# Attention of 48 steps in one sequence, both heads' scores side by side, and input weights split by an accumulating DMA

## The chip, the cores and the metric

The kernel runs on one core of a Trainium2 chip. The metric is the device time of one execution in microseconds (us), the median of several runs. The engines are TensorE (PE; its weight loads are listed apart as PEld), VectorE (DVE), ScalarE (ACT), GpSimd (POOL) and SyncE (SP). SP and POOL issue the DMAs, each in the order in which they stand in its own instruction stream.

## The reference, cut to what matters

One layer of a decoder trunk is computed for a prompt of 1024 tokens and 8 single-token samples, 1032 columns in all, with 1024 channels. One combined projection of the normalised input feeds a convolution branch, an attention branch and two gates:

```python
h = rms_norm(x, g_mix)
z = h @ w_in                                    # w_in: 1024 x 6400
a_lin, a_gate, q, k, v, g_a, g_b = jnp.split(z, SPLITS, axis=-1)
u = a_lin * jax.nn.sigmoid(a_gate)
c, new_conv = causal_dwconv(hist_conv, u, w_dw, b_dw)           # width 31
out_a = jax.nn.silu(layer_norm(c, ln_g, ln_b)) @ w_conv_out
q = rope(q.reshape(n_seq, t_len, N_HEADS, HEAD_DIM), pos) * (HEAD_DIM ** -0.5)
k = rope(k.reshape(n_seq, t_len, N_HEADS, HEAD_DIM), pos)
# three groups of four heads, window 128/512/2048, dilation 1/4/16:
s = jnp.einsum('brnqhd,brnkhd->brnhqk', qb, kb)                 # masked to the band
mx = jnp.max(s, axis=-1, keepdims=True)
p = jnp.exp(s - mx)
den = jnp.sum(p, axis=-1, keepdims=True)
o = jnp.einsum('brnhqk,brnkhd->brnqhd', p, vb) / den
# groups are weighted by their softmax sums, then out_b = o @ w_attn_out
x = x + (sigmoid(g_a) * out_a + sigmoid(g_b) * out_b) @ w_out
# then RMSNorm, the gated ConvFFN (up, conv of width 3, SiLU, down), residual, final RMSNorm
```

Each head has 64 channels, so two heads fill the 128 partitions of one block of q, k or v.

## The kernel before, in words

**Products.** Every large product is made of three passes in fp32r. A weight block of 128x1024 (`raw`) is split into a rounded high part `hi` and a rest `lo`; the activations are split likewise (`hh`, `hl`). `product` (L203) then adds `hi`·`hh`, `hi`·`hl` and `lo`·`hh` for eight channel blocks, 24 matmuls of 344 columns into one PSUM bank. `mm_blocks` (L219) makes three such banks, 3 x 344 columns, for one block of output channels; "job" below means one such weight block with its 72 matmuls. The pools hold `raw` twice and `hi` and `lo` three times (`WB` = 3), so a weight block can be split when the job three before it has ended.

**Loading weights.** `load_w` (L190) fetches `raw` from SP's queue; `split_w` (L180) makes `hi` by a copy on ACT and `lo = raw - hi` by a subtraction on DVE, with a raised priority.

**The stages.** After the first products come the input projections of the convolution, `ag` and `al` in turn (8 blocks each). A convolution of 31 taps for each of 8 channel blocks runs on DVE (`conv_wide`, L494: `ca<-cu,c_w_dw,ca`) from then until the gates. Then six attention units follow, numbered b = 0 to 5 (head group g = b // 2, pair of heads p = b % 2), each with a job of `q`, `k` and `v`; then the gates `ga` and `gb` (8 jobs each), the attention's output product `ob`, and the rest of the layer.

**Order.** `mm_blocks` calls `pump` (L125) after each bank: it takes steps from the queues `later` (attention), `second` and `third` (combining the groups, layer norm, the samples' output) and `taps` (convolution). So the source interleaves small work with the large products; from there a scheduler places each engine's instructions. `anchor` (L155) ties taps on DVE behind the last step of the work that PE needs.

**One attention unit.** `attention_unit` (L570) evacuates q, k and v on ACT, turns q and k by `rope` (L538: a STREAM_SHUFFLE and three or four operations of 1032 columns on DVE), and splits the 1024 tokens into eight blocks i = 0 to 7. `s20` is the score tile of unit 2, block 0. For each block there are three PE parts. `scores` (L603): for each of the two heads one score product in a bank of its own (tag `s`, two banks), each followed on DVE by a reduction that adds the mask and finds the maximum (`sm<-s`), and then one `nm` (minus the maximum) and two exponentials on ACT (`pr`). `turn` (L623): two or four transposes of the probabilities (`pt`), copied by ACT to `pk`. `weigh` (L633): two or four products with the values (`o`), copied by ACT to `ot`. `step(t)` of a unit (L644) runs `weigh(t-2)`, `turn(t-1)` and `scores(t)`, ten steps for a unit. These parts are in plain f32 and stand between the fp32r matmuls of the projections. `values` transposes v in two banks of tag `t`; the samples' scores (`products`, L676) use the bank of tag `o`.

## Time and profile before

| | us |
|---|---|
| time before, median of 3 runs (1661.45 to 1664.89) | 1663.66 |
| the profiled execution's own time | 1660.85 |
| its span in the trace | 1659.1 |
| PE busy in the span | 1616.9 |
| DVE busy | 1148.3 |
| ACT busy | 611.2 |
| POOL busy | 149.0 |

The span runs from the first to the last instruction of the profiled execution. A busy share is a mean over stages with different limits; a stretch of the trace says which engine was full there. A matmul's row gives its start and a modelled duration; since matmuls overlap, the cost of one is read from start to start.

### The profile page before, as it was taken

The page shows a single profiled execution, that of the slowest core. Times are in us where ns is not written, and L with a number is a line of the kernel's source. Part 1 is how long each engine was busy: PE and PEld are TensorE (multiplying, and loading weights), DVE is VectorE, ACT ScalarE, POOL GpSimd, SP SyncE. Part 2 cuts the span into 40 slices and gives each one's busy share as a digit, 9 for nine tenths or more (in the row PEclk, how much of TensorE's full clock was granted, in tenths as well). Part 3 has the DMA queues.
Part 4 walks back from the last instruction along what each step waited for, and adds up shares of the span by engine and source line. Part 5 has one row for each costly group of instructions (what it writes and reads, how often), then busy time and mean ns, then how long its engine had stood idle before and what let it go on. Part 6 is the DMA issues. An engine that isn't in the chain of part 4 may idle for free.

```text
span 1659.1 us, 26823 instructions
## 1 busy us (share of the span) xinstructions
PE 1616.9 (97%) x11044; PEld 1572.5 (95%) x11044; DVE 1148.3 (69%) x1778; ACT 611.2 (37%) x1080; POOL 149.0 (9%) x229
## 2 busy tenths in 40 slices
PE   8999999999999999999999989999999998999997
PEld 7999998899899999999999989999999998999997
DVE  5889998798986996774435886666666667434246
ACT  6421123444434323462223354444444444311123
POOL 0110011010102102120001000000000000000002
PEclk9999999999999999999999999999999999999999
DMA  8544332322325457894453135545545546762112
GB/s 292 182 133 125 97 116 83 84 87 87 116 90 194 130 179 229 231 349 142 174 217 107 60 94 155 166 135 146 166 134 147 140 115 249 257 218 87 57 34 102
DMA packets 84393, 244.94 MB, mean 148 GB/s; under 512 B 9840, under 2 KB 31376, under 8 KB 84272
## 3 DMA queue, kind: packets, MB, share of 16 engines
q1 hardware_dynamic: 61152, 163.09, 30.1%
q0 software_dynamic: 23120, 80.15, 15.9%
q8 instruction: 86, 1.41, 0.3%
q14 instruction: 35, 0.29, 0.1%
HBM read 195.87 MB, written 92.46 MB: 174 GB/s over the span
## 4 chain that ended last, share of the span: by engine, by line
PE 77%; DMA 12%; DVE 7%; issue 2%; ACT 2%; POOL 0%; SPq 0%; DVEq 0%; POOLq 0%; ACTq 0%
PE dn L215 12%; PE qb L1086 7%; DMA sa<-w_ups 7%; PE ga L215 6%; PE oa L215 5%; PE xo L215 5%; PE v L215 4%; PE k L215 4%; PE q L215 4%; PE al L215 4%; PE ag L215 3%; PE first L215 3%; PE qc L1086 3%; PE s L612 2%; PE dl L215 2%
## 5 line engine op out<-in xcount | busy, mean ns | idle before, releaser
L502 DVE SCALAR_TENSOR_TENSOR ca<-cu,c_w_dw,ca 128x1019 f32<-128x1019 f32 (+22 forms) x240 | 300.8, 1269 | 1.7
L215 PE MATMUL dn<-gh,hi_wd 128*128 128x344 f32 x456 | 146.2, 321 | 4.8 <-DVE xs L934 4.3
L215 PE MATMUL dn<-gl,hi_wd 128*128 128x344 f32 x456 | 145.7, 320 | 0.6 <-DVE gl L68 0.6
L215 PE MATMUL dn<-gh,lo_wd 128*128 128x344 f32 x456 | 146.1, 320 | 0.0
L934 DVE TENSOR_TENSOR xs<-dn,xs 128x1032 f32<-128x1032 f32 x34 | 41.7, 1230 | 117.5 <-PE dn L215 114.7
L1068 DVE TENSOR_TENSOR sb<-sa,raw_ra 128x512 f32<-128x512 f32 x20 | 13.9, 693 | 112.8 <-DMA sa<-w_ups 111.0
L215 PEld LDWEIGHTS dn<-gh,hi_wd 128*128 128x128 f32 x456 | 85.7, 188 | 6.2 <-DVE xs L934 4.6
L215 PEld LDWEIGHTS dn<-gl,hi_wd 128*128 128x128 f32 x456 | 85.7, 188 | 1.2 <-DVE gl L68 1.2
L215 PEld LDWEIGHTS dn<-gh,lo_wd 128*128 128x128 f32 x456 | 85.7, 188 | 0.0
L68 ACT ACTIVATE hi_wd<-raw_wd 128x768 fp32r<-128x768 f32 (+1 forms) x26 | 24.2, 929 | 135.9 <-PE dn L215 130.2
L215 PE MATMUL xo<-mh,hi_wo 128*128 128x344 f32 x192 | 62.3, 325 | 3.3 <-DVE xr L962 3.3
L1086 PE MATMUL qb<-t,hi_wd 128*128 128x258 f32 x320 | 59.3, 285 | 6.3 <-DVE uv18z L1121 1.3
L1086 PE MATMUL qb<-t,hi_wc 128*128 128x258 f32 x320 | 59.8, 287 | 5.1 <-ACT s L1137 5.1
L215 PE MATMUL ga<-hh,lo_ga 128*128 128x344 f32 x192 | 62.5, 325 | 0.0
L215 PE MATMUL ga<-hh,hi_ga 128*128 128x344 f32 x192 | 62.4, 325 | 0.0
L215 PE MATMUL ga<-hl,hi_ga 128*128 128x344 f32 x192 | 62.3, 325 | 0.0
L215 PE MATMUL xo<-ml,hi_wo 128*128 128x344 f32 x192 | 62.1, 324 | 0.0
L215 PE MATMUL gb<-hl,hi_gb 128*128 128x344 f32 x192 | 62.0, 323 | 0.0
L215 PE MATMUL xo<-mh,lo_wo 128*128 128x344 f32 x192 | 61.9, 323 | 0.0
L215 PE MATMUL gb<-hh,lo_gb 128*128 128x344 f32 x192 | 61.8, 322 | 0.0
L215 PE MATMUL oa<-sl,hi_wco 128*128 128x344 f32 x192 | 61.5, 320 | 0.0
L215 PE MATMUL oa<-sh,lo_wco 128*128 128x344 f32 x192 | 61.2, 319 | 0.0
(826 smaller groups left out, 5407.9 us busy)
## 6 DMA issues: line engine op xcount, KB each, us to landing
o_k<-cache_k SPq DMA_DIRECT2D x16, 1023.5 KB, 7.4
o_v<-cache_v SPq DMA_DIRECT2D x16, 1023.5 KB, 7.4
g<-g_dram SPq DMA_DIRECT2D x22, 516.0 KB, 7.3
sa<-w_ups SPq DMA_DIRECT2D x20, 512.0 KB, 3.7
sa<-w_ups POOLq DMA_DIRECT2D x20, 512.0 KB, 6.7
raw_ra<-w_ups SPq DMA_DIRECT2D x20, 512.0 KB, 3.6
raw_wd<-w_down SPq DMA_DIRECT2D x16, 384.0 KB, 3.1
rd<-w_ups SPq DMA_DIRECT2D x20, 256.0 KB, 3.5
```

Source lines behind the costliest of these rows:

```text
L68: ins = op(*args, **kwargs)
L215: ins = nc.tensor.matmul(ps[:, :m], wk, xk, start=(k == 0 and i == 0), stop=(k == n - 1 and i == 2))
L502: after(anchor[0], nc.vector.scalar_tensor_tensor(acc[:, d:SEQ], u[:, :SEQ - d], w[:, 30 - d:31 - d], acc[:, d:SEQ], ALU.mult, ALU.add))
L612: nc.tensor.matmul(sps[:, :nk], q[hs, i * P:(i + 1) * P], k[hs, k0:k0 + nk], start=True, stop=True)
L934: nc.vector.tensor_tensor(out=v3(t), in0=ps, in1=v3(t), op=ALU.add)
L1068: nc.vector.tensor_tensor(out=s2, in0=s1, in1=ra[:, 512:], op=ALU.add)
L1086: nc.tensor.matmul(ps[:, s, :SUB], wk, xk, start=(first and k == 0 and i == 0), stop=(k == 3 and i == 2), skip_group_check=True)
```

## The change

Three things change.

**The score tiles.** The two single banks of tag `s` become one tile of two banks (`two_banks`). Both heads' score products of a block go into it, one behind the other on PE; then come the two reductions. `values` and the transposes of the attention's output (`otr`) use the same tile with eight transposes and one evacuation; the samples' scores are put right behind the next block's scores, into its first bank. The tiles of the layer norm (`lm`, `sp_lv`) take the tags `s`, `t`, `o` in turn.

**The sequence.** The ten steps of each unit become one sequence of 48 steps over all units, with three more to empty it. Step n runs `weigh(n-3)`, `turn(n-2)` and `scores(n)`, tied in this order on PE. `ready` adds waits: no `weigh` or `turn` of step n starts before the exponentials of block n-2 are done on ACT (`exps`) and `nm` of step n-1 is done on DVE (`free[0]`).

**The loads.** For the 45 weight blocks that go through `in_jobs` (`ag`, `al`, `q`, `k`, `v`, `ga`, `gb`) `load_by_dma` takes the place of `load_w`: ACT writes `hi`, and then `-raw` rounded into `lo`; a DMA of 512 KB from POOL's queue adds the weight from DRAM to it. DVE's subtraction is gone. Other weights are split as before.

```diff
-PSA = {"mm": 4, "s": 2, "t": 1, "o": 1}
+PSA = {"mm": 4, "s": 1, "t": 1, "o": 1}
...
+    def two_banks(name):
+        return psb[0].tile([P, 2, 512], F32, tag="s", name=name, bufs=1)
...
+    def ready(first, then):
+
+        tc.add_manual_dep(
+            then.ins, first.ins.name,
+            mybir.DependencyInfo(mybir.DependencyClass.Sync, mybir.DependencyReason.DATA),
+            reason="together",
+        )
...
+    def load_by_dma(src, name):
+
+        raw, d = fetch_w(src, name)
+        hi, lo = w_tiles(name)
+        with tc.high_priority(EARLY):
+            act.activation(hi, raw, AF.Copy)
+            act.activation(lo, raw, AF.Copy, scale=-1.0)
+            nc.gpsimd.dma_start(lo, src, accum_op=ALU.add)
+        paced(d)
         return hi, lo
 
...
     def in_jobs(*jobs):
-        mm_blocks([(load_w(w_in[o], name), 0, name, ev) for o, name, ev in jobs], hh, hl)
+        mm_blocks([(load_by_dma(w_in[o], name), 0, name, ev) for o, name, ev in jobs], hh, hl)
...
         def values():
-            for half in range(2):
-                ps = bank(f"vtr{b}{half}", "t")
-                for i in range(4):
-                    o = (half * 4 + i) * P
-                    nc.tensor.transpose(ps[:, i * P:(i + 1) * P], vt[:, o:o + P], ident)
-                nc.scalar.activation(v[:, half * 4:half * 4 + 4, :], ps.rearrange("p (i c) -> p i c", c=P), AF.Copy)
+            ps = two_banks(f"vtr{b}")
+            for i in range(8):
+                nc.tensor.transpose(ps[:, i // 4, i % 4 * P:(i % 4 + 1) * P], vt[:, i * P:(i + 1) * P], ident)
+            nc.scalar.activation(v, ps.rearrange("p h (i c) -> p (h i) c", c=P), AF.Copy)
...
+        def scores(i, run, extra):
             nk, k0, prev = keys(i)
             mask = mask_d if g == 2 else (mask_b if prev else mask_b[:, P:])
             sm = scratch(f"sm{b}{i}", "sm").rearrange("p (h k) -> p h k", h=2)
             mx = ot[:, i, 2 * HALF:2 * HALF + 2]
             den = ot[:, i, 2 * HALF + 2:2 * HALF + 4]
+            sps = two_banks(f"s{b}{i}")
             for h in range(2):
-                sps = bank(f"s{b}{i}{h}", "s")
                 hs = slice(h * HALF, (h + 1) * HALF)
-                nc.tensor.matmul(sps[:, :nk], q[hs, i * P:(i + 1) * P], k[hs, k0:k0 + nk], start=True, stop=True)
+                after(run[0], nc.tensor.matmul(sps[:, h, :nk], q[hs, i * P:(i + 1) * P], k[hs, k0:k0 + nk],
+                                               start=True, stop=True))
+            for products in extra:
+                products(sps[:2 * NS, 0, 2 * P:3 * P + 1])
+            extra.clear()
+            for h in range(2):
                 nc.vector.tensor_tensor_reduce(
-                    out=sm[:, h, :nk], in0=sps[:, :nk], in1=mask, scale=1.0, scalar=-3e38,
+                    out=sm[:, h, :nk], in0=sps[:, h, :nk], in1=mask, scale=1.0, scalar=-3e38,
                     op0=ALU.add, op1=ALU.max, accum_out=mx[:, h:h + 1])
             nm = small.tile([P, 2], F32, tag="nm", name=f"nm{b}{i}")
-            anchor[0] = nc.vector.tensor_scalar(nm, mx, -1.0, None, ALU.mult)
+            anchor[0] = free[0] = nc.vector.tensor_scalar(nm, mx, -1.0, None, ALU.mult)
             probs[i] = scratch(f"pr{b}{i}", "pr").rearrange("p (h k) -> p h k", h=2)
             for h in range(2):
-                nc.scalar.activation(probs[i][:, h, :nk], sm[:, h, :nk], AF.Exp, bias=nm[:, h:h + 1],
-                                     accum_out=den[:, h:h + 1])
-
-        def turn(i):
+                exps[i] = nc.scalar.activation(probs[i][:, h, :nk], sm[:, h, :nk], AF.Exp, bias=nm[:, h:h + 1],
+                                               accum_out=den[:, h:h + 1])
+
+        def turn(i, run, gate):
             nk = keys(i)[0]
             tps = bank(f"pt{b}{i}", "t")
             for h in range(2):
                 for kb in range(nk // P):
                     o = h * nk + kb * P
-                    nc.tensor.transpose(tps[:, o:o + P], probs[i][:, h, kb * P:(kb + 1) * P], ident)
+                    ins = nc.tensor.transpose(tps[:, o:o + P], probs[i][:, h, kb * P:(kb + 1) * P], ident)
+                    for first in gate:
+                        ready(first, ins)
+                    after(run[0], ins)
+            run[0] = ins
             turned[i] = scratch(f"pk{b}{i}", "pk")
             nc.scalar.activation(turned[i][:, :2 * nk], tps[:, :2 * nk], AF.Copy)
 
-        def weigh(i):
+        def weigh(i, run, gate):
             nk, k0, _ = keys(i)
             ops = bank(f"o{b}{i}", "o")
             for h in range(2):
                 for kb in range(nk // P):
                     o = h * nk + kb * P
-                    nc.tensor.matmul(ops[:, h * HALF:(h + 1) * HALF], turned[i][:, o:o + P],
-                                     v[:, k0 // P + kb, h * HALF:(h + 1) * HALF],
-                                     start=(kb == 0), stop=(kb == nk // P - 1))
+                    run[0] = nc.tensor.matmul(ops[:, h * HALF:(h + 1) * HALF], turned[i][:, o:o + P],
+                                              v[:, k0 // P + kb, h * HALF:(h + 1) * HALF],
+                                              start=(kb == 0), stop=(kb == nk // P - 1))
+                    for ins in gate:
+                        ready(ins, run[0])
             nc.scalar.activation(ot[:, i, :2 * HALF], ops[:, :2 * HALF], AF.Copy)
 
-        def step(t):
-            if 0 <= t - 2:
-                weigh(t - 2)
-            if 0 <= t - 1 < 8:
-                turn(t - 1)
-            if t < 8:
-                scores(t)
+        parts = {"scores": scores, "turn": turn, "weigh": weigh, "exps": exps}
...
-            def products():
-                sps = bank(f"ss{b}", "o")
+            def products(sps):
                 for i in range(NS):
-                    nc.tensor.matmul(sps[:2 * NS, :P + 1], qb[:, i * 2 * NS:(i + 1) * 2 * NS], kc[:, i, :],
+                    nc.tensor.matmul(sps, qb[:, i * 2 * NS:(i + 1) * 2 * NS], kc[:, i, :],
                                      start=(i == 0), stop=(i == NS - 1))
...
-        later.extend([lambda: None] * (3 if b == 0 else 0))
+        later.extend([lambda: None] * (3 if not units else 0))
         later.append(values)
-        for t in range(10):
-            later.append(lambda t=t: step(t))
-            if t == 1:
-                later.append(lambda: later.insert(3, sample_scores()))
-        later.append(store)
+        units.append((parts, store))
+        for i in range(8):
+            later.append(lambda n=8 * len(units) - 8 + i: step(n))
+            if i == 1:
+                later.append(lambda: later.insert(3, lambda products=sample_scores(): extra.append(products)))
+
+    units, extra, free = [], [], [None]
+    STEPS = 6 * 8
+
+    def step(n):
+
+        run, gate = [None], []
+        part = lambda m: (units[m // 8][0], m % 8)
+        if 0 <= n - 2 < STEPS:
+            u, i = part(n - 2)
+            gate = [u["exps"][i], free[0]]
+        if 0 <= n - 3:
+            u, i = part(n - 3)
+            u["weigh"](i, run, gate)
+            if i == 7:
+                b = (n - 3) // 8
+                units[b][1]()
+                if b >= 4:
+                    second.append(combine(b - 4))
+        if 0 <= n - 2 < STEPS:
+            u, i = part(n - 2)
+            u["turn"](i, run, gate)
+        if n < STEPS:
+            u, i = part(n)
+            u["scores"](i, run, extra)
...
-            ps = bank(f"lm{c}", "s")
+            ps = bank(f"lm{c}", "sto"[c])
...
-        if g == 2:
-            later.append(lambda p=p: second.append(combine(p)))
+    for n in range(STEPS, STEPS + 3):
+        later.append(lambda n=n: step(n))
```

How the change moves instructions is shown at two places. The first is the start of unit 2, on PE and on DVE. Names carry the unit and the block behind the tile's letter: `s20` is the score tile of unit 2, block 0 (before, a third digit names the head), `o17` the output tile of unit 1, block 7; `k3_2` and `v3_1` are blocks of 344 columns of unit 3's projections. On PE before, around the scores of block 1:

```order
L215 MATMUL k3_1_3453<-hh3_96,hi_k3_3391 128x344
L639 MATMUL o16_3263<-vk1_2691,pk16_3203 128x64 x4
L594 MATMUL vtr20_3311<-c_ident_120,vr2_3219 128x128 x4
L215 MATMUL k3_1_3453<-hl3_104,hi_k3_3391 128x344
...
L215 MATMUL k3_2_3527<-hl1_102,hi_k3_3391 128x344
L639 MATMUL o17_3276<-vk1_2691,pk17_3274 128x64 x4
L594 MATMUL vtr21_3317<-c_ident_120,vr2_3219 128x128 x4
L612 MATMUL s210_3369<-k2r_3049,q2r_2852 128x256
L612 MATMUL s211_3372<-k2r_3049,q2r_2852 128x256
```

The output products of unit 1 stand apart from each other, and no wait ties them to unit 2's maxima. On PE in the change, from unit 2's first scores to the last output product of unit 1:

```order
L237 MATMUL v3_0_3531<-hh7_100,lo_v3_3527 128x344
L632 MATMUL s20_3301<-k2r_3001,q2r_2843 128x128 x2
L668 MATMUL o16_3339<-vk1_2636,pk16_3298 128x64 x4
L654 MATMUL pt17_3345<-c_ident_120,pr17_3246 128x128 x4
L632 MATMUL s21_3353<-k2r_3001,q2r_2843 128x256 x2
L237 MATMUL v3_1_3581<-hh0_93,hi_v3_3526 128x344
...
L237 MATMUL v3_2_3609<-hh2_95,hi_v3_3526 128x344
L668 MATMUL o17_3440<-vk1_2636,pk17_3350 128x64 x4
```

Now `s20` is followed at once by step 17 (`o16`, `pt17`, `s21`), whose first product waits for `nm20`; 31 matmuls of `v3` stand between `s21` and `o17`, which waits for `nm21`. On DVE before, between the same two maxima:

```order
L613 ISA sm20_3351,ot2_3226<-s201_3355,c_mask_band_794 128x128
L613 ISA ot2_3226 128x1
L540 STREAM_SHUFFLE q3p_3382<-q3t_3227 128x1032
L617 TENSOR_SCALAR nm20_3358<-ot2_3226 128x2
L541 TENSOR_TENSOR q3t_3227<-q3t_3227,rope_c_920 128x1032
L542 TENSOR_TENSOR q3p_3382<-q3p_3382,rope_s_921 128x1032
L547 TENSOR_TENSOR q3r_3386<-q3t_3227,q3p_3382 128x1024
...
L613 ISA sm21_3368,ot2_3226<-s211_3372,c_mask_band_794 128x256
L613 ISA ot2_3226 128x1
L617 TENSOR_SCALAR nm21_3375<-ot2_3226 128x2
```

And on DVE in the change:

```order
L638 ISA sm20_3300,ot2_3163<-s20_3301,c_mask_band_794 128x128
...
L562 STREAM_SHUFFLE q3p_3365<-q3t_3164 128x1032
L642 TENSOR_SCALAR nm20_3306<-ot2_3163 128x2
L524 SCALAR_TENSOR_TENSOR ca4_2995<-cu4_2993,c_w_dw_788,ca4_2995 128x1015
L563 TENSOR_TENSOR q3t_3164<-q3t_3164,rope_c_921 128x1032
L564 TENSOR_TENSOR q3p_3365<-q3p_3365,rope_s_922 128x1032
L524 SCALAR_TENSOR_TENSOR ca4_2995<-cu4_2993,c_w_dw_788,ca4_2995 128x1014
L638 ISA sm21_3352,ot2_3163<-s21_3353,c_mask_band_794 128x256
...
L569 TENSOR_TENSOR q3r_3369<-q3t_3164,q3p_3365 128x1024
...
L693 COPY kc2_3405<-k2r_3001 128x8
L562 STREAM_SHUFFLE k3p_3515<-k3t_3165 128x1032
L642 TENSOR_SCALAR nm21_3358<-ot2_3163 128x2
```

Two taps have moved in between, and the sum `q3r` and the next rope's shuffle `k3p` now stand between the reduction of `s21` and `nm21`. The same pattern stands at the starts of units 3 and 4, with the rope of units 4 and 5.

The second place is POOL's queue in the convolution's stage. Before, from the load of the second convolution's input on:

```order
L497 DMA cu1_1344<-u_dram1_800 128x1032
L499 TENSOR_SCALAR ca1_1346<-cu1_1344,c_w_dw_788,c_pvec_89 128x1024
L489 DMA u_dram2_801<-u2_816 128x1032
L490 DMA o_u<-u2_816 128x38
L489 DMA u_dram3_802<-u3_925 128x1032
```

And in the change:

```order
L208 DMA lo_al3_1026<-w_in 128x1024
L519 DMA cu1_1350<-u_dram1_800 128x1032
L521 TENSOR_SCALAR ca1_1352<-cu1_1350,c_w_dw_788,c_pvec_89 128x1024
L511 DMA u_dram2_801<-u2_816 128x1032
L512 DMA o_u<-u2_816 128x38
L208 DMA lo_ag4_1124<-w_in 128x1024
L208 DMA lo_al4_1217<-w_in 128x1024
L511 DMA u_dram3_802<-u3_926 128x1032
```

The new DMAs stand between stores and loads that wait for work of DVE, ACT or other DMAs; `lo_ag4` is behind the stores of `u2`.

## Rows read from the trace of the kernel before

**Rows 1.** One stretch: length; busy PE, PEld, DVE, ACT, POOL; clock; DMA share; GB/s.

```profile
237.00:572.00 335.00, 335.00 (x2165) 301.52 (x2164) 285.84 (x516) 131.46 (x385) 41.37 (x63) 1.00 0.33 103
```

**Rows 2.** PE's waits from 560 to 760 us: total, times, longest.

```profile
PE ob L215 <- DVE sb L833: 1.7, 2, 1.3
```

**Rows 3.** Timeline of PE: start, duration, then the instruction.

```profile
245.97 0.31 PE L215 MATMUL k<-hl,hi_k 128*128 128x344 f32 x1
246.21 0.70 PE L612 MATMUL s<-k0t,q0t 64*128 64x256 f32 x4
246.85 0.42 PE L215 MATMUL k<-hh,lo_k 128*128 128x344 f32 x1
...
251.28 0.32 PE L215 MATMUL k<-hl,hi_k 128*128 128x344 f32 x1
251.44 0.32 PE L215 MATMUL k<-hh,lo_k 128*128 128x344 f32 x1
251.69 0.70 PE L612 MATMUL s<-k0t,q0t 64*128 64x256 f32 x2
252.32 0.43 PE L215 MATMUL k<-hh,hi_k 128*128 128x344 f32 x1
252.59 0.32 PE L215 MATMUL k<-hl,hi_k 128*128 128x344 f32 x1
...
334.87 1.00 PE L639 MATMUL o<-vk,pk 128*128 128x64 f32 x8
...
336.88 0.42 PE L215 MATMUL q<-hl,hi_q 128*128 128x344 f32 x1
...
370.17 0.33 PE L215 MATMUL v<-hh,lo_v 128*128 128x344 f32 x1
370.43 0.49 PE L612 MATMUL s<-k2r,q2r 64*128 64x128 f32 x4
370.85 0.43 PE L215 MATMUL v<-hh,hi_v 128*128 128x344 f32 x1
...
381.70 0.31 PE L215 MATMUL v<-hh,hi_v 128*128 128x344 f32 x1
381.94 0.48 PE L612 MATMUL s<-k2r,q2r 64*128 64x128 f32 x2
382.36 0.42 PE L215 MATMUL v<-hl,hi_v 128*128 128x344 f32 x1
```

**Rows 4.** Timeline of DVE in unit 3's rope.

```profile
371.87 1.32 DVE L540 STREAM_SHUFFLE k3p<-k3t 128x1032 f32<-128x1032 f32 x1
373.08 0.16 DVE L617 TENSOR_SCALAR nm<-ot 128x2 f32<-128x2 f32 x1
...
376.61 1.27 DVE L502 SCALAR_TENSOR_TENSOR ca<-cu,c_w_dw,ca 128x1010 f32<-128x1010 f32 x1
377.79 0.42 DVE L613 CUSTOM_DVE_ANT_0 sm<-s,c_mask_band 128x256 f32<-128x256 f32 x1
...
378.48 2.02 DVE L547 TENSOR_TENSOR k3r<-k3t,k3p 128x1024 f32<-128x1024 f32 x1
...
380.48 0.18 DVE L617 TENSOR_SCALAR nm<-ot 128x2 f32<-128x2 f32 x1
382.58 0.29 DVE L613 CUSTOM_DVE_ANT_0 sm<-s,c_mask_band 128x128 f32<-128x128 f32 x1 [1.91 <-PE s L612]
```

**Rows 5.** DVE's groups: count, busy us, mean ns, idle before.

```profile
L68 DVE TENSOR_TENSOR lo_ga<-raw_ga,hi_ga 128x1024 fp32r<-128x1024 f32 x8 | 9.7, 1217 | 8.0 <-ACT hi_ga L68 8.0
```

**Rows 6.** The page's DMA issues: count, KB each, median us to landing.

```profile
sa<-w_ups POOLq DMA_DIRECT2D x20, 512.0 KB, 6.7
```

**Rows 7.** Timeline around the split of `ag4` and its first use.

```profile
94.11 1.06 ACT L68 ACTIVATE hi_ag<-raw_ag 128x1024 fp32r<-128x1024 f32 x1 [4.32 <-PE al L215]
...
95.64 0.56 POOL L490 DMA_DIRECT2D o_u<-u  x1
...
105.09 0.32 PE L215 MATMUL ag<-hh,hi_ag 128*128 128x344 f32 x1
```

More of the change, by code (lines that the diff above doesn't have):

```diff
@@ L187, in split_w @@
             dve.tensor_tensor(out=lo, in0=raw, in1=hi.bitcast(F32), op=ALU.subtract)
+        return hi, lo
+    def load_by_dma(src, name):
[6 more added lines that the diff above has]
+        paced(d)
         return hi, lo
@@ L278, in token_rstd, with spread @@
         return rsqrt(ps, [t[:, i, :ps.shape[-1]] for i in range(3)])
-    def spread(r, name, behind=None, n=CW, d=None):
+    def spread(r, name, behind=None, n=CW, d=None, tag="s"):
         offs = offsets(n)
@@ L290, in spread @@
         )
-        ps = bank(f"sp_{name}", "s")
+        ps = bank(f"sp_{name}", tag)
         for j, off in enumerate(offs):
@@ L599, in keys @@
             return (2 * P if prev else P), ((i - 1) * P if prev else i * P), prev
-        probs, turned = {}, {}
-        def scores(i):
+        probs, turned, exps = {}, {}, {}
+        def scores(i, run, extra):
             nk, k0, prev = keys(i)
@@ L744, in combine @@
             yield
-        for half in range(2):
-            ps = bank(f"otr{p}{half}", "t")
-            for i in range(4):
-                nc.tensor.transpose(ps[:, i * P:(i + 1) * P], os_[0][:, half * 4 + i, :], ident)
-            sl = slice(half * 512, half * 512 + 512)
-            split(ps, oT_h[:, sl], oT_l[:, sl])
-            yield
+        ps = two_banks(f"otr{p}")
+        for i in range(8):
+            nc.tensor.transpose(ps[:, i // 4, i % 4 * P:(i % 4 + 1) * P], os_[0][:, i, :], ident)
+        split(ps.rearrange("p a b -> p (a b)"), oT_h[:, :SEQ], oT_l[:, :SEQ])
+        yield
         third.append(sample_out(p))
@@ L782, in layer_norm @@
         for c in ALL:
-            ps = bank(f"lm{c}", "s")
+            ps = bank(f"lm{c}", "sto"[c])
             nc.tensor.matmul(ps[:, :CW], onesm, c_sum[:, cs(c)], start=True, stop=True)
             nc.scalar.activation(mub[:, cs(c)], ps[:, :CW], AF.Copy, scale=1.0 / DM)
-            yield
+        yield
         vs = scratch("vs", "ln", T)
@@ L802, in layer_norm @@
         for c in ALL:
-            nc.scalar.activation(rb[:, cs(c)], spread(rl[:, 3 * c:3 * c + 3], f"lv{c}"), AF.Copy)
-            yield
+            nc.scalar.activation(rb[:, cs(c)], spread(rl[:, 3 * c:3 * c + 3], f"lv{c}", tag="sto"[c]), AF.Copy)
+        yield
         for k in range(KB):
```

2 lines of the change are left out of this document (1 added, 1 removed).

## The prediction

> **What bounds the kernel now.** I read the stretches first, then the waits, then the timeline of PE and DVE inside one of those stretches. In the stretch of the six attention units, from 237 to 572 us, PE is busy in all of its 335 us, while DVE has 285.84 and ACT 131.46 [rows 1]. So in this stage time is PE's time: what shortens the list of its instructions is a gain, one for one, and what makes it wait is a loss, one for one. DVE is the engine that could make it wait, with 85% of the stretch taken. ACT has room. DVE is often ahead: it sat 1.91 us before a reduction, waiting for its scores [rows 4]. Behind this stage PE also has few gaps; one that this change touches is at the attention's output product, where PE waits 1.7 us for DVE's `sb` [rows 2].
>
> The sum is made against the profiled execution, 1660.85 us, which is 2.8 under the median of 1663.66. I move the result by that much at the end. About 0.2%, 3.3 us, is what a measurement of this kernel can tell from no change.
>
> **Heads side by side (gain).** An fp32r matmul of 344 columns takes 0.16 us from start to start (251.28 to 251.44). Between two of them, one head's 256-wide scores take from 251.44 to 252.32, 0.88 us; both heads' adjacent take from 245.97 to 246.85, also 0.88 us. For 128 columns it is 0.66 us for one head (381.70 to 382.36) and 0.68 for both (370.17 to 370.85) [rows 3]. The second head is free as long as it follows the first directly. The fp32r matmul behind such a run also takes 0.27 us instead of 0.16 (252.32 to 252.59). So a run of scores of its own costs 0.88 + 0.27 - 2 x 0.16 = 0.83 us at 256 columns, and in the same way 0.61 at 128. In the trace I count 48 blocks; in 12 of 256 columns and 11 of 128 the two heads stand apart. In the change's order all 48 stand together. The gain is 12 x 0.83 + 11 x 0.61 = 16.7 us.
>
> **Fewer runs (gain).** Plain f32 work of the attention stands in 125 runs between fp32r matmuls; in the change's order there are 54. Apart from the 23 split heads that is 48 entries fewer. Each entry costs the 0.11 us of the slower fp32r matmul behind it [rows 3], but a switch inside a run, from output products to transposes to scores, may cost as much. Bounds are 0 and 5.3 us; I take half, 2.6. Together with the heads PE's list is 19.3 us shorter.
>
> The Trainium skill, in TensorEngine Tiling (Array Packing), section Key Properties, says that a change of tiling mode drains TensorE. By that rule the two halves of a 64-row pair would be cheap and each entry dear, so the term would lie at its upper bound and the sum 2.7 us lower; the rows above can't separate the two.
>
> **The new waits (loss).** `ready` makes the first PE instruction of step n wait for `nm` of step n-1. I walked through the 48 steps in the change's order, with PE's pitches above and DVE's: a tap and a rope product, 3.53 us for three of them (373.08 to 376.61), a tap 1.18, two reductions 0.69 at 256 columns, a rope's sum and its short tail 2.00 (378.48 to 380.48), a shuffle 1.21 (371.87 to 373.08) [rows 4]. In 39 of the steps 4 to 9 us of fp32r matmuls cover DVE. Not so at the starts of units 2, 3 and 4, where the order puts rope work between the reductions and `nm`:
> - `o16` follows `s20` at once. DVE's reduction starts 0.16 us after the scores' end (381.94 + 0.48 to 382.58), two of 128 columns take some 0.5, then the shuffle 1.21 and `nm` 0.1: PE stands 2.0 us. Nothing can fill in: `v3_1` needs a free bank, and the evacuation of `k3_0` stands on ACT behind `pk17`.
> - From `nm20` to `nm21` DVE has two taps and two rope products (3.53 + 1.18), two reductions 0.69, the sum 2.00, a small copy and the shuffle 1.21: 8.8 us. PE has `o16`, `pt17` and `s21`, 2.1 us as in the run from 334.87 to 336.88 with its 0.11 [rows 3], and 31 fp32r matmuls, 4.9: 7.0. It stands 1.8 us (2.2 in unit 3).
> - Before the third step 0.2 to 1.1 us are left in the same way.
>
> That is 4.1 us in unit 2, 5.2 in unit 3 and 4.2 in unit 4, 13.5 in all. The last unit has no rope behind it and no such wait; before, the same DVE order cost nothing, since no PE work was tied to `nm`. The bounds are 0, if DVE's pitches or PE's overlap differ, and some 25 if each wait is twice that.
>
> **The loads.** 45 subtractions of 1.22 us leave DVE [rows 5], 55 us in all; DVE bounds no stage here, so this gives nothing by itself, but without it the walk above would have had longer waits. ACT gets 45 copies of 1.06 us [rows 7], 48 us, beside PE, in the stretch above 18 of them on top of 131 us of 335: hidden. If an ACT copy stood before an evacuation that PE waits for, it would cost up to 1.06 us each, 19 us for the 18; the order shows them mostly in the gaps behind `hi`. The accumulating DMA has a near row: the same form and size from POOL's queue takes 6.7 us to landing [rows 6]. A weight block is split when the job three before has ended, two jobs of 72 x 0.157 = 11.3 us ahead of its use, 22.6 us; copies and landing take about 10. Only the first blocks are closer. For `ag4` `hi` starts at 94.11, two copies end at 96.2, POOL has issued the stores ahead of it by 96.2 (95.64 + 0.56), the DMA lands near 103.5, and PE's first use is at 105.09 [rows 7]. `ag3` has about as little. I put 1 us on these, with bounds 0 and 4.
>
> The Trainium skill, in DMA: Bandwidth & Descriptors, section Anatomy of one DMA — SWDGE (gpsimd) path, gives 2.0 us plus bytes over 436e3 per us; worked out for 512 KB that is an estimate of 3.2 us, against 6.7 in the row. By the page the 1 us would be nothing; by the row it stands.
>
> **The end of the attention (gain).** In the change's order the last convolution sums, the layer norm and the samples' output come about one `gb` block earlier on PE, so I take the 1.7 us of waits at `ob` [rows 2] as gone; bounds 0 and 1.7. Values, `otr` and the layer norm's banks change no number of PE's instructions; their longer evacuations lie beside PE.
>
> **Sum.** -19.3 + 13.5 + 1.0 - 1.7 = -6.5 us, 1654.4 against the profiled 1660.85, and 1657 against the median.
>
> **Rivals.**
> - *The waits are mostly hidden.* The walk puts PE against DVE with a margin of 2 us at each place, from durations of another execution. If DVE, rid of its subtractions, stands half a tap earlier in each of these steps, half of the waits fall away; if the reductions come out first, all do. Then -14 to -20 us: 1644 to 1650. For it: DVE's slack seen above. Against it: at the unit starts the rope itself lies between, and no lead helps where `s20` is followed by `o16` at once.
> - *The waits eat the gain.* As the walk, but a further 0.17 us in each of the 39 other steps, from taps that have just begun when the scores end: 39 x 0.17 = 6.6 us. Then no change: 1660 to 1667.
> - *Slower: PE and DVE in lock step.* Before, the score products of two heads had two banks, and `o` and `pt` no tie to the newest scores. Now each step needs DVE to have finished the step before. If DVE's share of 85%, less 18 x 1.22 us, is spread so that a tap or a rope piece stands before the reduction in most steps, each step waits 0.6 us: 48 x 0.6 = 29 us, less 21 gained: +8, 1671. It decides from a mean wait of 0.45 us in a step. Against it: the 5 to 6 us of fp32r work between two steps.
> - *Slower: the accumulating DMAs come late.* POOL issues in order, and they stand between stores and loads that wait for convolution and attention. It costs nothing until one is held up by 12 us (22.6 less 10); from there each job waits in full, and five jobs late by 2 us are 10 us: 1667 to 1670. A store is issued in 0.56 us while DVE runs taps [rows 7], which speaks against a slow queue. The Trainium skill, in SBUF — State Buffer, section Who interferes with whom, says that DVE copies in a two-port mode lock GpSimd's descriptor writing out; no run here shows it.
>
> **How the numbers follow.** The walk as it stands, -3 to -12 us: 0.43. Waits mostly hidden: 0.22. Gain eaten, within 3.3 us: 0.20. Lock step 0.10 and late loads 0.05. Faster by over 0.2% has 0.65, within it 0.20, slower 0.15. The time is that of the first, 1657. Its own range is 1651 to 1661. Both signs hold chance, so the range reaches from 1644, all waits hidden, to 1668, the gain eaten and a little more.
>
> **What the profile will show.** Right: all score rows of both heads adjacent, plain f32 runs of about 54 in the stretch; PE waiting on DVE's `nm` at `o16`, `o17`, `o20` and the like in units 3 and 4, near 2 us each and 13 in all; no wait of PE on a `lo` DMA past `ag4`; ACT near 660 us and DVE near 1093. Wrong: waits on `nm` in many more steps, or in none; PE waiting for weights; or a stage behind `oa` that changes its length.

## The result and the profile after

The changed kernel takes 1679.66 us (median of 4 runs, 1675.19 to 1680.67) against 1662.56 for before (4 runs; the three known when the forecast was made gave 1663.66): ratio 1.0093, 95% interval 1.0071 to 1.0114. It is slower by 17 us; 1657 and a range of 1644 to 1668 were forecast.

The profiled execution took 1680.67 us, its span is 1678.9. I cut both traces at the first matmul of `q`, of `ga` and of `oa`, the first products of the units, of the gates and of the convolution's output:

| stretch of PE | before, us | after, us | difference | forecast |
|---|---|---|---|---|
| start to first `q` | 195.7 | 196.8 | +1.1 | +1.0 |
| first `q` to first `ga` (attention units) | 298.6 | 292.2 | -6.4 | -5.8 |
| first `ga` to first `oa` (gates, end of attention, layer norm) | 234.2 | 253.1 | +18.9 | -1.7 |
| first `oa` to the end | 930.6 | 936.8 | +6.2 | 0 |

Read by stretch, the units went as forecast and the loss lies behind them. But the stretches do not hold the same work. The same cuts before (length; busy PE, PEld, DVE, ACT, POOL, each with its count; clock; DMA share; GB/s):

```profile
195.70:494.30 298.60, 298.60 (x1929) 270.39 (x1927) 263.32 (x441) 110.95 (x313) 34.00 (x50) 1.00 0.32 96
494.30:728.50 234.20, 231.70 (x1482) 224.23 (x1481) 184.00 (x350) 92.01 (x174) 43.97 (x73) 1.00 0.63 201
```

and in the change:

```profile
196.80:489.00 292.20, 283.03 (x1868) 263.94 (x1867) 221.34 (x377) 120.55 (x296) 49.40 (x62) 0.98 0.49 127
489.00:742.10 253.10, 242.14 (x1542) 234.96 (x1541) 184.96 (x375) 109.97 (x214) 57.66 (x91) 0.97 0.78 224
```

Some 60 matmuls, all of them the attention's, have moved from the units behind the first `ga`: the -6.4 is in part their leaving, and in the +18.9 they come back. So I also read both stretches together: 545.3 us against 532.8, 12.5 more, where 7.5 less was forecast. PE's waits in them are 20 us against 2.5. The granted clock is at the lower of its two levels (1.2 GHz) for some 27 us against none (length times twice what the clock lacks to 1.00). At that level a matmul of 344 columns takes 0.29 us instead of 0.16 (rows below), so the 27 us cost some 12, an estimate. What then remains, some -17 us, is PE's shorter list. Two stretches at the same times say it in other words, first in the changed kernel:

```profile
237.00:572.00 335.00, 325.60 (x2178) 301.77 (x2178) 246.04 (x468) 148.03 (x395) 60.61 (x81) 0.98 0.51 134
572.00:700.00 128.00, 118.37 (x716) 116.21 (x716) 87.95 (x169) 45.57 (x70) 27.92 (x44) 0.93 0.85 238
```

and the second of them before:

```profile
572.00:700.00 128.00, 127.80 (x823) 126.85 (x821) 95.23 (x183) 41.58 (x66) 21.49 (x39) 1.00 0.70 219
```

Where PE was full before [rows 1] it now has 9.4 us of gaps, and DVE does 40 us less in the same time, some 24 of them the 20 subtractions that are gone [rows 5]. Between 572 and 700 us, where PE had 127.80 of 128 us before at full clock, it has 118.37 at a mean granted clock of 0.93, and does 716 matmuls instead of 823. The six largest waits of PE between 71 and 760 us in the changed kernel (total, times, longest); before, that stretch held 2.5 us, most of it [rows 2]:

```profile
PE o L668 <- DVE nm L642: 8.4, 6, 2.1
PE otr L796 <- DVE o L787: 3.7, 1, 3.7
PE gb L237 <- DMA lo_gb<-w_in: 2.6, 1, 2.6
PE ga L237 <- ACT sa L575: 1.7, 2, 1.5
PE tm_lv L282 <- DVE vs L328: 1.3, 1, 1.3
PE sp_lv L315 <- DVE diag_lv L68: 1.1, 1, 1.1
```

The first line is the wait that the prediction priced; the next five were not in it. Together they are 18.8 us. The start of unit 3 shows the first line's wait, on PE:

```profile
416.46 0.32 PE L237 MATMUL v<-hh,lo_v 128*128 128x344 f32 x1
416.71 0.49 PE L632 MATMUL s<-k3r,q3r 64*128 64x128 f32 x4
419.28 0.63 PE L668 MATMUL o<-vk,pk 128*128 128x64 f32 x4 [2.08 <-DVE nm L642]
...
421.57 0.65 PE L237 MATMUL v<-hh,hi_v 128*128 128x344 f32 x1
422.02 0.49 PE L237 MATMUL v<-hl,hi_v 128*128 128x344 f32 x1
422.31 0.49 PE L237 MATMUL v<-hh,lo_v 128*128 128x344 f32 x1
...
423.65 0.32 PE L237 MATMUL v<-hl,hi_v 128*128 128x344 f32 x1
423.81 0.32 PE L237 MATMUL v<-hh,lo_v 128*128 128x344 f32 x1
```

and on DVE:

```profile
417.36 0.29 DVE L638 CUSTOM_DVE_ANT_0 sm<-s,c_mask_band 128x128 f32<-128x128 f32 x1 [5.44 <-PE s L632]
...
417.79 1.29 DVE L562 STREAM_SHUFFLE q4p<-q4t 128x1032 f32<-128x1032 f32 x1
418.98 0.15 DVE L642 TENSOR_SCALAR nm<-ot 128x2 f32<-128x2 f32 x1
```

The scores of both heads are one run, as expected. The reduction starts 0.16 us after them, the rope's shuffle stands between it and `nm`, and PE waits 2.08 us; 2.0 were forecast. Behind the wait the granted clock falls, to 0.52 in the mean of 420 to 423 us. A matmul of 344 columns then takes 0.29 us from start to start (422.02 to 422.31), instead of 0.16, until 423.46. The wait at `otr` shows the clock in a longer stretch. The stretches around it (columns as above):

```profile
590.00:594.00 4.00, 4.00 (x28) 4.00 (x27) 4.00 (x5) 2.01 (x2) 0.51 (x1) 1.00 0.02 8
594.00:598.00 4.00, 1.09 (x7) 0.80 (x6) 4.00 (x6) 0.00 (x0) 3.60 (x5) 0.95 0.91 203
598.00:602.00 4.00, 1.97 (x8) 1.57 (x8) 3.93 (x4) 1.22 (x2) 0.00 (x0) 0.50 1.03 323
602.00:606.00 4.00, 3.79 (x13) 3.80 (x14) 3.96 (x4) 1.21 (x4) 0.57 (x1) 0.50 1.05 303
606.00:610.00 4.00, 4.00 (x22) 4.00 (x21) 2.71 (x4) 0.46 (x1) 0.00 (x0) 0.77 0.73 230
610.00:614.00 4.00, 4.00 (x28) 4.00 (x27) 3.79 (x9) 1.83 (x3) 0.00 (x0) 1.00 0.02 8
```

PE stands for 3.7 us until 598.8, and from 598 to 606 the granted clock is 0.50, its lower level; it is back at 1.00 by 610. At full clock PE does 28 matmuls in 4 us here; in the 16 us from 594 to 610 it did 50 instead of 112. The Trainium skill, in TensorE: Matmul & The Clock Gate, Part 1, says that the gate falls to 1.2 GHz when PE has been idle and rises once it is busy again. The trace agrees: 0.50 behind the 3.7 us, 1.00 again from 610 us on.

A third place is late data. POOL's queue, and then PE, in `gb`:

```profile
661.12 1.04 POOL L811 DMA_DIRECT2D pb<-pp_dram  x2 [14.10 <-DVE so L814]
662.16 0.92 POOL L208 DMA_DIRECT2D lo_gb<-w_in  x1
```

```profile
672.65 0.31 PE L237 MATMUL gb<-hl,hi_gb 128*128 128x344 f32 x1
675.57 0.43 PE L237 MATMUL gb<-hh,lo_gb 128*128 128x344 f32 x1 [2.60 <-DMA lo_gb<-w_in]
```

The accumulating DMA could have gone at 651.1, when its copy on ACT had ended. It stood in POOL's queue behind a load for the samples' output, which waited 14.10 us for DVE. So it was issued 11 us late, and it took until 675.5, 13.4 us, to land. In this stretch (640 to 705 us, DMA share 0.95) the median of the three of its kind was 11.4 us, and that of all 45 in the change 8.1, against 6.7 in [rows 6].

### The profile page after: what moved, and what is told of

It is laid out like the page before. It is cut to its first block, busy times and chain, and to the rows that moved or that the text cites. A ratio compares the mean times of both kernels' runs of the same rounds, so it can differ in the third digit from the quotient of the medians.

```text
span 1678.9 us, 26946 instructions
## 1 busy us (share of the span) xinstructions
PE 1616.6 (96%) x11044; PEld 1581.5 (94%) x11044; DVE 1101.3 (66%) x1731; ACT 650.9 (39%) x1117; POOL 189.5 (11%) x274
## 4 chain that ended last, share of the span: by engine, by line
PE 72%; DMA 14%; DVE 9%; issue 4%; ACT 2%; POOL 0%; SPq 0%; DVEq 0%; POOLq 0%; ACTq 0%
PE dn L237 12%; PE qb L1133 8%; DMA sa<-w_ups 6%; PE oa L237 5%; PE xo L237 5%; PE al L237 4%; PE ga L237 4%; PE k L237 4%; PE q L237 3%; PE first L237 3%; PE qc L1133 3%; PE v L237 3%; PE ag L237 3%; PE up L237 2%; DMA vc<-vT 2%
## 5 line engine op out<-in xcount | busy, mean ns | idle before, releaser
L524 DVE SCALAR_TENSOR_TENSOR ca<-cu,c_w_dw,ca 128x1009 f32<-128x1009 f32 (+19 forms) x240 | 301.0, 1268 | 3.0
L645 ACT ACTIVATE pr<-sm,nm 128x128 f32<-128x128 f32 (+1 forms) x96 | 42.4, 443 | 98.3 <-DVE nm L642 94.8
L1107 POOL DMA_DIRECT2D sa<-w_ups x20 | 17.4, 872 | 410.9 <-DVE lo_wd L68 210.0
L237 PE MATMUL gb<-hh,hi_gb 128*128 128x344 f32 x192 | 62.6, 326 | 0.6 <-ACT sb L875 0.6
```

Source lines behind the costliest of these rows:

```text
L237: ins = nc.tensor.matmul(ps[:, :m], wk, xk, start=(k == 0 and i == 0), stop=(k == n - 1 and i == 2))
L524: after(anchor[0], nc.vector.scalar_tensor_tensor(acc[:, d:SEQ], u[:, :SEQ - d], w[:, 30 - d:31 - d], acc[:, d:SEQ], ALU.mult, ALU.add))
L645: exps[i] = nc.scalar.activation(probs[i][:, h, :nk], sm[:, h, :nk], AF.Exp, bias=nm[:, h:h + 1], accum_out=den[:, h:h + 1])
L1107: nc.gpsimd.dma_start(sa, src[:, 1024:], accum_op=ALU.add)
```

## The experiments

Each kernel ran beside the kernel before. Ratios are to before, with 95% intervals. The stretches in the accounts are those of the table above, from the profiled execution of each, and they too can differ in the attention's work that they hold. A profiled execution is one of the runs: those of runs 7, 9 and 11 took 4 to 5 us more than the median, that of run 8 took 5 us less.

**1. The loads alone.** The kernel before, with `load_by_dma`:

```diff
-        mm_blocks([(load_w(w_in[o], name), 0, name, ev) for o, name, ev in jobs], hh, hl)
+        mm_blocks([(load_by_dma(w_in[o], name), 0, name, ev) for o, name, ev in jobs], hh, hl)
```

> The attention of before, with only the input weights' low parts by accumulating DMA. Theory A (the loss is PE's new waits behind the attention's new order, each followed by a stretch at half clock): near before, 1660 to 1667 us, with at most the one wait on a late lo of gb, 3 us and its slow stretch. Rival B (the 23.6 MB of new DMAs on POOL's queue make the loss, by lateness and by traffic): 1673 us or more.

1670.3 us, ratio 1.0030 (1.0018 to 1.0043). Above the range of theory A, below that of B. The units gained 6 us (292.6): the scheduler, with DVE freer, put 36 of 48 pairs of heads together instead of 25. From `ga` to `oa` it lost 10 (244.4). The waits of PE between 71 and 760 us:

```profile
PE tm_lv L271 <- DVE vs L317: 7.3, 1, 7.3
PE gb L226 <- ACT sb L839: 2.2, 2, 1.8
PE ob L226 <- DVE sbr L844: 1.1, 2, 0.8
```

`tm_lv` is the layer norm's variance. PE waits for DVE's sum there, which waits for the loads `cn` of the convolution's output; in POOL's queue these stand among eight accumulating DMAs for `gb` and the loads `pb`, which wait for DVE. So the loads alone are a small loss, and in this trace it comes with POOL's order and not with PE waiting for a weight.

**2. The attention alone.** The change, with `load_w` in `in_jobs` again:

```diff
-        mm_blocks([(load_by_dma(w_in[o], name), 0, name, ev) for o, name, ev in jobs], hh, hl)
+        mm_blocks([(load_w(w_in[o], name), 0, name, ev) for o, name, ev in jobs], hh, hl)
```

> The changed attention, with the low parts by DVE's subtraction as before. Theory A: slower than before too, 1668 to 1680 us, with waits of PE on DVE at o and otr no shorter than in the change, since DVE has 55 us more to do. Rival B: faster than before, 1655 us or less.

1681.5 us, ratio 1.0102 (1.0080 to 1.0123), 1.5 us above theory A's range and far from B's. The attention's part makes the loss, with waits of 9.3 us at `o`, 6.4 at `otr` and 5.1 at `sp_lv`. In the change the loads give no more than the 1.9 us between the two.

**3. No added waits.**

```diff
-            gate = [u["exps"][i], free[0]]
+            gate = []
```

> The change without the added waits (gate empty); the data's own waits remain. Theory A: the waits at o (8 us and some 3 of slow matmuls) go, those at otr and in gb stay or move: 1664 to 1672 us. Theory C (without the gates PE meets the same late data at pt and s, so that the waits are only renamed): 1676 to 1682 us.

1651.7 us, ratio 0.9920 (0.9901 to 0.9940): 28 us faster than the change, more than either theory had. The units take 282.4 us, 16.2 less than before, and PE waits nowhere in them. The waits are not renamed. One of 4.8 us is left, at `tm_lv`; those at `otr` and on `lo_gb` are gone as well. So the added waits cost much more than the time that PE stands at them.

**4. Heads side by side alone.** The kernel before, with one tile for both heads (and, as in the change, the layer norm's tiles in the tags `s`, `t`, `o`):

```diff
+            sps = two_banks(f"s{b}{i}")
             for h in range(2):
-                sps = bank(f"s{b}{i}{h}", "s")
...
-                nc.tensor.matmul(sps[:, :nk], q[hs, i * P:(i + 1) * P], k[hs, k0:k0 + nk], start=True, stop=True)
+                nc.tensor.matmul(sps[:, h, :nk], q[hs, i * P:(i + 1) * P], k[hs, k0:k0 + nk], start=True, stop=True)
+            for h in range(2):
```

> Before, with one change: both heads' scores of a block in one tile of two banks, one behind the other, then both reductions; steps, loads and the rest as before. In its order 41 of 48 pairs stand together instead of 25. By the price of a head that stands apart (0.83 and 0.61 us) 16 pairs give 10 to 13 us: 1649 to 1653 us. If the single score tile makes PE wait for DVE's reductions instead, 1660 us or more, with waits at s.

1659.1 us, ratio 0.9969 (0.9953 to 0.9985). The units take 285.5 us, 13.1 less than before, and `ga` to `oa` 242.2, 8.0 more, 4 of them a wait of `ob` for DVE's `sbr`. But 46 of the attention's matmuls have moved from the one into the other. Over both, the gain is 5.1 us; with 1.8 us more of waiting and 10 us at the lower clock (some 4.6) taken out, PE's list is some 11.5 us shorter, which is within the 10 to 13 of the price of a head. The total missed.

**5. Only the wait on the exponentials.**

```diff
-            gate = [u["exps"][i], free[0]]
+            gate = [u["exps"][i]]
```

> The change with one of its two added waits: a step's products wait for the exponentials of block n-2, not for nm of step n-1. Theory D (the wait on nm makes the loss, since it ties each step to the newest work of DVE): as without both waits, 1649 to 1656 us. Theory E (either wait holds the attention back): 1660 us or more.

1647.0 us, ratio 0.9899 (0.9875 to 0.9922); measured again (run 12) 1647.0, ratio 0.9902. As theory D, 2 us under its range. The wait on `nm` of the step before is the whole loss: 32.7 us between this kernel and the change. In the traces 9.9 lie in the units (292.2 against 282.3) and 21.1 from `ga` to `oa` (253.1 against 232.0; 18.6 against run 12's 234.5). The second figure holds 46 of the attention's matmuls that the units of the change no longer have. Over both stretches the difference is 31.0 us: 18.6 of it are PE's waits, and some 11 the lower clock (27 us against 3.4). PE's only wait between 71 and 760 us that is left:

```profile
PE tm_lv L282 <- DVE vs L328: 1.4, 1, 1.4
```

DVE shows the other side. Its waits from 196 to 600 us, in the change:

```profile
DVE sm L638 <- ACT pk L660: 48.2, 17, 5.4
DVE sm L638 <- PE s L632: 24.7, 7, 6.1
```

and without the wait on `nm`:

```profile
DVE sm L638 <- PE s L632: 37.0, 12, 5.9
DVE sm L638 <- ACT pk L660: 15.8, 4, 4.2
```

`sm` is the reduction over new scores. DVE stands before it for 72.9 us in the change and 53.2 without the wait (0.4 of them in a line not shown). The profile names ACT's `pk` for many; in the last row below, `pk` (a copy of that step's transposes) and the scores ended at 540.75 and 540.69, so either way DVE stood for PE's step. This idle time is not the price of the wait, though. With the subtractions back, it is 42.7 us with both added waits (run 2) and 37.4 without (run 8), and yet those kernels are 19 us apart; before, it was 35.3. In the last unit of the change it looks like this on DVE:

```profile
531.12 2.58 DVE L524 SCALAR_TENSOR_TENSOR ca<-cu,c_w_dw,ca 128x1015 f32<-128x1015 f32 x2
535.67 0.29 DVE L638 CUSTOM_DVE_ANT_0 sm<-s,c_mask_diag 128x128 f32<-128x128 f32 x1 [1.97 <-ACT pk L660]
...
536.22 0.17 DVE L642 TENSOR_SCALAR nm<-ot 128x2 f32<-128x2 f32 x1
540.85 0.29 DVE L638 CUSTOM_DVE_ANT_0 sm<-s,c_mask_diag 128x128 f32<-128x128 f32 x1 [4.46 <-ACT pk L660]
```

`nm` is followed by the next block's reduction, with no tap between, so DVE idles 4.46 us until PE has come to the next scores. In PE's order, the steps themselves stand later too: the output of unit 4's last block stands in `ga2` in the change and in `ga1` without the wait, that of unit 5 in `ga5` and in `ga4`. In time the last output product starts at 577.6 us against 543.4, and the last of the convolution's sums on DVE at 631.5 against 600.6. In the kernel before they start at 566.0 and 631.9: the convolution is late only against run 5.

**6 and 7. The waits in one half of the steps.** Both waits up to step 33 and none after, and the reverse:

```diff
+            gate = [u["exps"][i], free[0]] if n < 34 else []
```

> The change with both added waits up to step 33 (the starts of units 2, 3 and 4), none after. Theory F (half of the loss is made at the unit starts, half by the attention's late end, which reaches the combination of the groups): three waits of 2.35 us at unit starts with their slow stretches, 8 to 12 us over the kernel without the waits, 1659 to 1664 us, and no wait at otr. Theory G (the unit starts are all of it): 1672 us or more.

> The change with the added waits from step 34 on only. Theory F: no wait at the starts of units 2 to 4, the wait at otr of 3 to 6 us with its slow stretch, and late work in gb: 1664 to 1672 us. Theory G: as without the waits, 1649 to 1655 us.

1671.6 us, ratio 1.0042 (1.0028 to 1.0055), and 1656.9, ratio 0.9963 (0.9947 to 0.9980). Both times lie within 2 us of theory G and outside theory F, but the stretches fit neither, and runs 9 and 10 speak against G. With the first half the units take 292.3 us and `ga` to `oa` 245.2, 10 and 13 more than without the wait on `nm`. With the second half alone the units take 278.2, and `ga` to `oa` 248.3, 16 more, with waits at `otr` (1.1 us), on `sb` (3.2), `tm_lv` (2.7) and on `lo_gb` (1.6). Either half makes a loss behind the units, the early steps too, when the later ones are free.

**8. No added waits, low parts by subtraction.** The kernel of run 3 with the edit of run 2:

```diff
+            gate = []
...
+        mm_blocks([(load_w(w_in[o], name), 0, name, ev) for o, name, ev in jobs], hh, hl)
```

> The changed attention without the added waits, and the low parts by DVE's subtraction as before. Theory H (the new DMAs in POOL's queue hold up the loads of the layer norm's input, so that tm_lv waits): the wait at tm_lv (4.8 us with its slow stretch) goes, 1642 to 1649 us. Theory I (DVE's 55 us of subtractions are missed: DVE comes late): 1655 us or more.

1662.2 us, ratio 0.9988 (0.9972 to 1.0003). As theory I: without the accumulating DMAs the kernel of run 3 loses 10.5 us. In the profiled executions, 7.6 us apart, 7.3 lie from `ga` to `oa` (244.1 against 236.8), with waits of 4.0 us at `sp_lv` and 1.9 at `tm_lv` for DVE. So DVE's relief is worth much without the added waits, though the loads alone (run 1) were a loss and in the change they give next to nothing (run 2).

**9 and 10. The unit starts.** The wait on `nm` in the nine steps at the starts of units 2, 3 and 4 alone, and in all but these:

```diff
+            gate = [u["exps"][i], free[0]] if n in (17, 18, 19, 25, 26, 27, 33, 34, 35) else [u["exps"][i]]
```

> The wait on nm kept in nine of the 48 steps alone, the first three at the starts of units 2, 3 and 4; the wait on the exponentials in all. Theory K (the prediction's own: PE's waits at the unit starts are the loss): 1672 us or more. Theory L (the wait on nm in all steps makes PE and DVE take turns, DVE stands idle for scores, the convolution on it falls behind, and that is paid at otr and in gb): no more than half of the loss, 1652 to 1662 us.

> The reverse: the wait on nm in all steps but those nine. Theory K: 1645 to 1653 us, as without that wait. Theory L: DVE still idles some 15 us more before the reductions than without the wait, and the waits at otr and in gb stay: 1664 us or more.

1653.5 us, ratio 0.9944 (0.9923 to 0.9965), and 1678.1, ratio 1.0083 (1.0061 to 1.0104). The times are theory L's, against the prediction's own walk. With the wait at the starts alone the order no longer puts `o16` right behind `s20` (32 matmuls lie between), and no line of PE waiting for `nm` is left. So run 9 shows that the scheduler can avoid these waits, not what they cost. With the wait everywhere else, DVE idles 74.7 us before its reductions, and the loss is what it was.

**11 and 12. The best version.** The kernel of run 5, with the eight `gb` weights split by subtraction; beside it run 5 again:

```diff
+        load = load_w if jobs[0][0] >= 42 else load_by_dma
```

> As the run with the wait on the exponentials alone (1647), but the eight gb weights split by DVE's subtraction again. If the accumulating DMAs in POOL's queue hold up the layer norm's loads in gb: tm_lv waits no more and 2 to 4 us are gained, 1643 to 1646 us. If DVE, which is behind there, is the limit: 1648 to 1653 us.

> The same kernel as the run with the wait on the exponentials alone, timed in more rounds beside the others of this call: 1645 to 1650 us.

1643.0 us, ratio 0.9875 (0.9854 to 0.9896), and 1647.0. PE has no wait left between 71 and 760 us, and `ga` to `oa` takes 228.6 us, the least of all. It is faster than before by 20 us and than the change by 36. The intervals of the two overlap a little, so the last 4 us are likely and not certain.

**13 and 14. DVE's share.** The change and the kernel of run 5, both with 10 of the 30 taps left out in the last three convolution blocks:

```diff
-        for d in range(1, 31):
+        for d in range(1, 21 if j > 4 else 31):
```

> The change, with 10 of the 30 taps on DVE left out in each of the last three convolution blocks (part of the convolution is not computed), 35 us less for DVE from unit 5 on. Theory M (behind the units the loss is that DVE's convolution is late): the waits at otr, tm_lv and sp_lv go, and only the unit starts' 10 to 12 us stand against the same cut without the wait on nm: 1653 to 1662 us. Theory N (the late end of the attention itself makes the loss, whatever DVE has to do): 1667 us or more.

> The control: the same cut in the kernel with the wait on the exponentials alone. No PE wait is left there that 35 us of DVE could shorten but 1 to 3 us at tm_lv: 1641 to 1648 us.

1676.1 us, ratio 1.0079 (1.0056 to 1.0102), and 1648.0, ratio 0.9915 (0.9885 to 0.9945). Theory M falls: 35 us less for DVE give the change 3.5 us. The convolution's last sum comes at 582.3 instead of 631.5, the wait at the first `otr` goes, and others take its place:

```profile
PE o L668 <- DVE nm L642: 9.2, 8, 2.1
PE otr L796 <- issue: 4.0, 1, 4.0
PE tm_lv L282 <- DVE vs L328: 2.6, 1, 2.6
PE gb L237 <- ACT sb L875: 2.4, 2, 1.8
```

The `otr` that waits now is the second, at 625 us. Its input comes from unit 5's output, which left PE at 575.0 and was fetched again by POOL only from 595.0 on: ahead of it in POOL's queue stand a load `pb` for the samples' output, which waited 10.1 us for DVE, and a `lo_gb`.

**15. More taps per step** in the change (2.3 instead of 2).

```diff
-RATES = (2.6, 2)
+RATES = (2.6, 2.3)
```

> The change with all its work and more taps taken per step in the units (2.3 instead of 2), which puts them into the stretches in which DVE idles for scores. Theory M: the convolution ends some 10 us earlier, the waits at otr and in gb shrink: 1667 to 1676 us. Theory N: 1678 us or more.

1673.8 us, ratio 1.0063 (1.0038 to 1.0087). The size that theory M gave: `ga` to `oa` 246.9 instead of 253.1, the convolution's end at 613.4. With run 13 beside it, DVE's lateness is a part of some 4 to 6 us and not the whole.

**16 and 17. An earlier end.** Steps are taken in pairs from 7 waiting entries on, in the change and in the best version:

```diff
-LD = 9
+LD = 7
```

> The change, both waits kept, but steps of the attention are taken from their queue in pairs from 7 waiting entries on instead of 9, so that the last output product stands four blocks of ga earlier on PE. Theory N (the late end of the attention brings the combination and the layer norm late): the stretch from ga to oa shrinks by 10 us or more, the unit starts' waits stay: 1660 to 1669 us. Theory M (DVE's lateness alone): 1674 us or more.

> The kernel with the wait on the exponentials alone and gb's weights by subtraction (1643), with the same earlier taking of steps. It has no wait of PE left in gb, so an earlier end gives nothing there: 1640 to 1646 us; 1648 or more if the steps crowd DVE.

1681.6 us, ratio 1.0103 (1.0070 to 1.0135), and 1650.2. Theory N missed. The first time is in theory M's range, but by what follows it is no point for M either. In the order the last output product stands in `ga4` instead of `ga5`; in time it starts at 568.0, only 9.6 us earlier, since the steps now wait on `nm` in `ga` too (8.1 us there, up to 4.0 at a time, of 13.3 in all), and `tm_lv` waits 8.3. With the wait on `nm` in place, moving the steps earlier turns into waiting for DVE. In the best version it costs 7 us; its trace has PE waiting 2.9 us at `sp_lv` and 1.3 in `ga`, and the rest stays open.

## Why the prediction was wrong

- **Heads and runs (-19.3).** Right. All 48 pairs stood together in the change. With the waits and the estimate for the clock taken out of both stretches, PE's list is some 17 us shorter in the change and some 19 in runs 3, 5, 11 and 12, against 11.5 for the pairs alone in run 4, where 41 of 48 stand together.
- **The new waits (+13.5).** Right in place, and in size for the first wait of each unit: three of 2.08 us or a little less, where 2.0 was forecast. The later ones were forecast at 7.5 us and came to 2.1, all in unit 3. Behind each first wait PE ran at its lower clock, 10 us in the units altogether, and so came later itself. That clock cost some 4.6 us, which the prediction did not price: 8.4 of waits and 4.6 of clock are near 13.5 by luck, and the -6.4 of the units against -5.8 is luck too, since some 60 matmuls had left them.
- **The loads (+1.0).** +1.1 up to the first `q`. Behind that a step failed: "it costs nothing until one is held up by 12 us". That allowed 10 us for copies and landing. In `gb` POOL's queue held one up by 11 us, its landing took 13.4 us instead of 6.7, and PE waited 2.6 us. The late-loads rival, at 0.05, had this mechanism. The other direction, what the DMAs hold up behind them in the queue (`cn`, seen in run 1), I had not considered. "This gives nothing by itself", of the subtractions, held in the change (run 2) and not without the added waits (run 8: 10.5 us).
- **The end of the attention (-1.7).** This is the step that failed: "the last convolution sums, the layer norm and the samples' output come about one `gb` block earlier on PE, so I take the 1.7 us of waits at `ob` as gone". The waits at `ob` did go, but the stretch grew by 18.9 us: PE's waits in it are 11 us instead of 2.5, and the clock is low for 17 us, some 7.7 us of time; the rest is attention work that has moved in. I read PE's order there and did not ask whether DVE, ACT and POOL would have the data by then. `tm_lv` stands 38 matmuls of `gb` earlier on PE than before, half a block, and starts 8 us later in time. And I did not see that the attention's own end moves back: the first `otr` stands 123 matmuls of `ga` later than before and still met its data too early, since the last output product of unit 4 came 25 us later (534.6 against 509.7).
- **The clock (not in the sum).** This is the largest part of the miss: the sum prices each wait by its length alone and puts what follows it at nothing, without a reason. The two stretches missed the forecast by 20 us: 12 of them are the lower clock behind the waits, 6 are more waiting than forecast (20 us against 2.5, so 17.5 more, where 13.5 less 1.7 was forecast), and 2 a smaller gain in the list.
- **Which rival.** "Lock step" at 0.10 was nearest, with 1671 against 1679.7. Its tie was right: each step needs DVE to have finished the step before. Its price was wrong: it looked for 0.6 us of waiting on PE in each step. PE waits in six steps; the attention as a whole ends 34 us later than without the tie, and the price is paid behind the units and in the clock.

That the wait on `nm` makes the loss is shown by runs 3, 5 and 10. What the loss is made of on PE is accounted for above; how each wait behind the units comes about is shown only in part. Run 13 gives 3.5 us and run 15 some 6 for relief of DVE's convolution, and a `lo_gb` late in POOL's queue costs some 4 with its slow stretch. That the rest follows from the late end of the attention fits most runs: without the wait the last output product starts 65 us behind the first `ga` and the stretch takes 232 us, with it 89 and 253, and runs 6, 7 and 9 lie between. Run 15 (90 and 247) fits less well, and run 16, made to move that end alone, didn't move it enough to decide. The wait also changes the order that the scheduler makes; waiting and order were not told apart, since no kernel was made with the one and not the other. Behind `oa`, with PE's instructions in the same order, the +6.2 us are of the same two kinds: 1.9 us more of waiting, and 26.6 us at the lower clock against 16.9, some 4.4 us of time. Why the same order drew more of both is open; in all 18 other profiled executions that part takes 933.1 to 939.1 us, and 930.6 in the one of before.

## What to carry to other kernels

A wait that ties a step to the newest result of another engine costs more than the time at the wait: here it moved the end of the attention back by 34 us, and the bill came where other work was due. Price a wait on a full PE with the slow stretch behind it, which here added some 12 us to 20 us of waits. Follow each late product (here a store, a reload, a sum) to the place where PE meets it. When an edit moves work on the bound engine, check for each operand which engine and which queue delivers it, and what stands ahead of it there. And before two stretches are compared, count their instructions: a cut at a named product need not hold the same work.

## What the runs showed of the hardware

After a single wait of 2.08 us, in the middle of an otherwise full PE, the granted clock was 0.52 in the mean of 420 to 423 us, and matmuls of 344 columns took 0.29 us instead of 0.16. After one of 3.7 us at `otr` it was 0.50 for 8 us. In the change PE ran at the lower level for some 27 us between the first `q` and the first `oa`; before, with 2.5 us of waits there, it never did. An accumulating DMA of 512 KB, 6.7 us to landing in the median of [rows 6], took 8.1 in the median of the 45 of the change, and 11.4 in that of the three between 640 and 705 us, where the DMA share was 0.95.
